# One block of a hybrid encoder on one core: the transfers and gate products of the recurrent branch change engine, and a reciprocal is made in two

## The chip, the core and the metric

The kernel runs on one core of a Trainium2 chip. The time is device microseconds of one launch. A launch computes one layer of a hybrid encoder block for 256 tokens of width 2048, with all weights (some 190 MB in fp32) read once from HBM.

## The reference, cut to what matters

```python
def hybrid_layer(x, mem, ...):
    h = rms_norm(x, norm_g)
    proj = h @ w_in                                  # 256x2048 @ 2048x16512
    (aq, ak, av, az, br, bk, bv, bz, bwd, bad, cq, cz, ga, gb, gc) = split(proj)
    ya = chunked_band_attention(rms_norm(aq), rms_norm(ak), av, a_rel_bias) * silu(az)
    yb = rwkv7_time_mix(br, bk, bv, bwd, bad, ...) * silu(bz)      # 16 heads of 64
    mk, mv = split(rms_norm(mem) @ w_mem_kv)
    yc = memory_cross_attention(rms_norm(cq), rms_norm(mk), mv) * silu(cz)
    merged = sigmoid(ga)*(ya @ w_up_a) + sigmoid(gb)*(yb @ w_up_b) + sigmoid(gc)*(yc @ w_up_c)
    return x + merged @ w_o

def rwkv7_time_mix(...):          # the recurrent branch, per head, over 256 steps
    kk = kk * rsqrt(max(sum(kk*kk), 1e-24))
    # state = state*w_t + (state a_t) b_t + v_t k_t ;  out_t = state r_t
    o = rwkv7_scan(r, decay, k, v, -kk, kk * a)
    o = (o - mean) * rsqrt(var + GN_EPS) * ln_w + ln_b             # per head
    return o + sum(r*k*r_k) * v
```

## The kernel before

**The weight stream.** All weights lie in one HBM array of 186 chunks of 128x2048 fp32 (1 MB). `wload` (L170 to L180) fetches a chunk into a tile `raw` (two buffers) by a DMA that SyncE issues (L175). `wchunk` splits it into two halves and each half into a rounded part and a remainder: ScalarE casts `whi` (L185), VectorE subtracts to get `wlo` (L187); both have four buffers. TensorE then makes twelve matmuls for a half (L204 and L205 with `whi`, L209 with `wlo`; L222, L223 and L225 in the projections that come out transposed). The whole program is 370 such half steps, one after another, and everything else is laid between them.

**The branches as generators.** Attention, cross-attention, transposes and the recurrent branch are Python generators. After each half step `tick()` advances every generator by one yield, so a `yield n` means that the next piece is written n half steps later. The order of the instructions on each engine is then set by a scheduler that sorts all of them; each engine and each engine's DMA queue works its list strictly in that order.

**The recurrent branch** (`rwkv`, L507 to L789) runs for four groups q of four heads. In each:

- L524 to L548: sigmoids of the decay and the learning rate, and ScalarE's square of `kk` into a tile with the tag `tmpA` (one buffer);
- L554 to L559: the norm of `kk`, with a reciprocal over 128x512 on VectorE (L557);
- L577 to L587: the tiles AX, BK and `rk2`;
- L598 to L615: score matmuls, masked into TT;
- L622 and L626: TT goes to an HBM scratch in four DMAs (`scrt`) and comes back as `Tu`, 32x32 triangular systems spread over the partitions;
- L633 to L637: VectorE solves them in 31 steps; L644 and L645 write the result X to HBM twice, L666 to L671 read it back in eight DMAs (D0, D1T and XT, whose tag is `kk`);
- L690 and L699: two small rounds of matmuls; then the state is carried over four chunks c (L712 to L764; L719, L726, L735, L749 are its matmuls, and VectorE copies between them, L721, L729);
- after chunks 1 and 3 the output is normalised per head on GpSimd (L779 to L789). The scale and the shift `lw` come from HBM into a tile of tag `tmpA` (L771) and are read by GpSimd in L785 and L786. L789 adds into `vL`.

All DMAs of this branch but a small weight are issued by SyncE, in one list with the weights. After the branch four products on VectorE (L933 and L934) multiply `vL` by a gate into `zb`, which TensorE transposes (L325).

GpSimd's own DMAs before are the attention bias (L840, 256 rows of 1 KB), the residual input and the output (L954 and L959, 128 rows of 2 KB).

Of the kernel before, what the change touches and what calls it, by code (L numbers as in the profile page):

```python
# [11 lines left out]
ALU = mybir.AluOpType  # L12
# [6 lines left out]
P = 128  # L19
# [74 lines left out]
def _build(ctx, nc, tc, A, out, dbg):  # L94
# [14 lines left out]
    V, SC, G, T = nc.vector, nc.scalar, nc.gpsimd, nc.tensor  # L109
# [8 lines left out]
    def t(pl, shape, tag, dtype=F32, bufs=1):  # L118
        return pl.tile(shape, dtype, name=nm(tag), tag=tag, bufs=bufs)
# [319 lines left out]
    vL = t(vp, [P, 2, 1024], "vL")  # L439
# [36 lines left out]
    rp = pool(rk_st, "rwkv", side="right")  # L476
# [30 lines left out]
    def rwkv(q, w2a2, r_, k_):  # L507
# [44 lines left out]
        rn = t(rp, [P, 2, S], "tmpB")  # L552
# [1 line left out]
        V.tensor_scalar(out=rn2, in0=ssp, scalar1=1e-24, scalar2=None, op0=ALU.max)  # L554
        SC.activation(rn2, rn2, AF.Sqrt)
        yield 2
        V.reciprocal(rn2, rn2)  # L557
        yield 1
        V.tensor_tensor(out=kk, in0=kk, in1=rn, op=ALU.mult)  # L559
        k2 = t(rp, [P, 2, S], "tmpA")  # L560
        for b in range(2):
# [56 lines left out]
        for par in range(2):  # L618
            for b in range(2):
                u0 = (par * 2 + b) * 8  # L620
                r0 = par * 64 + b * 32
                nc.sync.dma_start(scr_t[u0:u0 + 8].rearrange("g s t -> s g t"),  # L622
                                  TT[r0:r0 + 32, :, :, b * 32:b * 32 + 32].rearrange("p b c t -> p (b c) t"))
        yield 1
        Tu = t(rp, [P, 32, 32], "Tu")
        nc.sync.dma_start(Tu.rearrange("p a b -> p (a b)"),  # L626
                          bass.AP(tensor=scr_t.tensor, offset=scr_t.offset, ap=[[1024, 32], [0, 4], [1, 1024]]))
        X = t(rp, [P, 32, 8], "Xu")
        V.tensor_copy(X.rearrange("p a b -> p (a b)"), eye8)
        yield 4  # L630
        tm = t(rp, [P, 192], "tmu")
        for s in range(31):
            n, m = 31 - s, min(s + 1, 8)  # L633
# [7 lines left out]
        V.tensor_copy(Xt, X.rearrange("p a b -> p b a"))  # L641
        scr_x = dr.tile([P, 256], F32, name=nm("scrx"), tag="scrx", bufs=2)
        scr_xt = dr.tile([P, 256], F32, name=nm("scrxt"), tag="scrxt", bufs=2)
        nc.sync.dma_start(scr_x, X.rearrange("p a b -> p (a b)"))  # L644
        nc.sync.dma_start(scr_xt, Xt.rearrange("p a b -> p (a b)"))  # L645

        BKt = t(rp, [P, 2, 3, P], "BKt")
        for b in range(2):
# [2 lines left out]
                T.transpose(bt[:, c, :], BK[:, b, c].rearrange("p a u -> p (a u)"), ident)  # L651
            SC.copy(BKt[:, b], bt)

        yield 1
        XT = t(rp, [P, 8, 64], "kk")
        D0 = t(rp, [P, 8, 32], "D0")
        D1T = t(rp, [P, 8, 32], "D1T")
# [1 line left out]
        for par in range(2):  # L659
            r0 = par * 64  # L660
            ua, ub = par * 16, par * 16 + 8

            def xt_src(u):
                return bass.AP(tensor=scr_xt.tensor, offset=scr_xt.offset + u * 1024, ap=[[32, 32], [1024, 8], [1, 32]])

            nc.sync.dma_start(D0[r0:r0 + 32].rearrange("p g c -> p (g c)"),  # L666
                              bass.AP(tensor=scr_x.tensor, offset=scr_x.offset + ua * 1024,
                                      ap=[[8, 32], [256, 32], [1, 8]]))
            nc.sync.dma_start(D1T[r0:r0 + 32], xt_src(ub))
            nc.sync.dma_start(XT[r0:r0 + 32, :, 0:32], xt_src(ua))  # L670
            nc.sync.dma_start(XT[r0 + 32:r0 + 64, :, 32:64], xt_src(ub))  # L671
        yield 5

        UV = t(rp, [P, 4, 2, 2, 64], "Tu")
        SV = t(rp, [P, 4, 2, 2, 64], "BK")
# [34 lines left out]
        for c in range(4):  # L710
            yield 1
            tt, ro = c // 2, (c % 2) * 64  # L712
            chn = psum([P, 3, 2, 64])
            for b in range(2):
                for par in range(2):
                    rs = slice(par * 64, par * 64 + 64)
                    ot = slice(64 - par * 64, 128 - par * 64)
                    kr = ot if c == 0 else slice(0, P)
                    T.matmul(chn[rs, 0, b, :], AX[kr, b, c, 2 * par, :], SV[kr, c, par, b, :], start=True, stop=True)  # L719
            rhs = t(rp, [P, 2, 64], "rhs")  # L720
            V.tensor_copy(rhs, chn[:, 0])  # L721
            yield 1
            for b in range(2):
                for par in range(2):
                    rs = slice(par * 64, par * 64 + 64)
                    T.matmul(chn[rs, 1, b, :], XT[rs, b * 4 + c, :], rhs[rs, b, :], start=True, stop=True)  # L726
            for par in range(2):
                rs = slice(par * 64, par * 64 + 64)
                V.tensor_copy(UV[rs, c, par], chn[rs, 1])  # L729
            yield 1  # L730
            if c < 3:
                for b in range(2):
                    for par in range(2):
                        rs = slice(par * 64, par * 64 + 64)
                        T.matmul(chn[rs, 2, b, :], BKt[:, b, c, par * 64:par * 64 + 64], UV[:, c, par, b, :],  # L735
                                 start=True, stop=True)
            if c % 2 == 1:
                ob = psum([P, 4, 64])
                for b in range(2):
                    for cc in (c - 1, c):  # L740
                        if cc > 0:
                            oc = slice((cc % 2) * 64, (cc % 2) * 64 + 64)
                            T.matmul(ob[oc, b * 2:b * 2 + 2, :].rearrange("p h i -> p (h i)"), AX[:, b, cc, 1, :],
                                     S0z[cc % 2][:, b].rearrange("p h i -> p (h i)"), start=True, stop=False)
                    for par in range(2):
                        h = b * 2 + par
                        for cc in (c - 1, c):
                            oc = slice((cc % 2) * 64, (cc % 2) * 64 + 64)
                            T.matmul(ob[oc, h, :], RR[:, h, cc, :], UV[:, cc, par, b, :], start=(cc == 0),  # L749
                                     stop=(cc == 0 or par == 1))  # L750
            if c < 3:
                fb = fx[:, :, c].unsqueeze(2).to_broadcast([P, 2, 64])
                t1 = t(rp, [P, 2, 64], "st1")
                if c == 0:
                    V.tensor_copy(t1, chn[:, 2])  # L755
                else:
                    V.tensor_tensor(out=t1, in0=chn[:, 2], in1=S0n, op=ALU.add)
                for par in range(2):
                    rs = slice(par * 64, par * 64 + 64)
                    V.tensor_tensor(out=SV[rs, c + 1, par], in0=t1[rs], in1=fb[rs], op=ALU.mult)  # L760
                    G.tensor_tensor(out=S0z[(c + 1) % 2][rs, :, par], in0=t1[rs], in1=fb[rs], op=ALU.mult)  # L761
                if c < 2:
                    S0n = t(rp, [P, 2, 64], "s0n")
                    G.tensor_tensor(out=S0n, in0=t1, in1=fb, op=ALU.mult)  # L764
            if c % 2 == 1:
                bon = psum([P, 2, P])
                for b in range(2):
                    T.matmul(bon[:, b, :], rk2[:, b, tt * P:tt * P + P], BO, start=True, stop=True)
                lw = t(rp, [P, 2, 256], "tmpA")
                for i in range(2):  # L770
                    nc.sync.dma_start(lw[:, i, :], bass.AP(tensor=A["bc"].tensor, offset=(1 + i) * 1024 + q * 256,  # L771
                                                             ap=[[0, P], [1, 256]]))
                mean = t(sm, [P, 4], "mean", bufs=2)
                V.tensor_reduce(out=mean, in_=ob, axis=AX_X, op=ALU.add)
                V.tensor_scalar(out=mean, in0=mean, scalar1=1.0 / 64, scalar2=None, op0=ALU.mult)
                cen = t(rp, [P, 4, 64], "D0")
                V.tensor_tensor(out=cen, in0=ob, in1=mean.unsqueeze(2).to_broadcast([P, 4, 64]), op=ALU.subtract)
                cq = t(rp, [P, 4, 64], "D1T")
                G.tensor_tensor(out=cq, in0=cen, in1=cen, op=ALU.mult)  # L779
                var = t(sm, [P, 4], "var", bufs=2)  # L780
                V.tensor_reduce(out=var, in_=cq, axis=AX_X, op=ALU.add)
                rsqrt_small(var, var, 4, 1.0 / 64, GN_EPS)
                G.tensor_tensor(out=cen, in0=cen, in1=var.unsqueeze(2).to_broadcast([P, 4, 64]), op=ALU.mult)
                c2 = cen.rearrange("p h i -> p (h i)")
                G.tensor_tensor(out=c2, in0=c2, in1=lw[:, 0, :], op=ALU.mult)  # L785
                G.tensor_tensor(out=c2, in0=c2, in1=lw[:, 1, :], op=ALU.add)  # L786
                bv = t(rp, [P, 256], "M1")
                V.tensor_tensor(out=bv, in0=bon.rearrange("p b s -> p (b s)"), in1=vL[:, tt, tokc], op=ALU.mult)
                G.tensor_tensor(out=vL[:, tt, tokc], in0=c2, in1=bv, op=ALU.add)  # L789
# [140 lines left out]
    finish(rwg)  # L930
    rk_st.close()
    for tt in range(2):
        V.tensor_tensor(out=zb[:, tt, 0:512], in0=vL[:, tt, 0:512], in1=zb0[:, tt, :], op=ALU.mult)  # L933
        V.tensor_tensor(out=zb[:, tt, 512:1024], in0=vL[:, tt, 512:1024], in1=zb[:, tt, 512:1024], op=ALU.mult)  # L934
    dump("y_b", zb)
    g_st = ExitStack()
    gp = pool(g_st, "gb")
# [84 lines left out]
```

## Time and profile before

| | |
|---|---|
| runs of the kernel | 1186.29 us median of 3 (1185.37 to 1188.55) |
| profiled execution | 1184.23 us, span 1182.5 us |
| mean granted TensorE clock | 0.996 of full speed |
| busy: TensorE, VectorE, ScalarE, GpSimd | 1154.7, 778.8, 531.3, 122.5 us |
| moved by DMA | 217.93 MB, 184 GB/s over the span |

The profiled execution lies 1.7 us above its span and 2.1 us under the median of the runs. PE stands for TensorE, DVE for VectorE, ACT for ScalarE, POOL for GpSimd, and SPq for the list of DMAs that SyncE issues. An arrow in a wait reads: who waited, and for what. Small matmuls keep PE counted as busy, so what a stall costs is read from the windows and the waits, not from the share alone.

### The profile page before, as it was taken

To read this page: it belongs to the slowest core of one execution; us is meant where nothing else is said; L and a number is where in the kernel's file an instruction comes from. 1 tells how busy PE (TensorE), PEld (TensorE's weight loads), DVE (VectorE), ACT (ScalarE), POOL (GpSimd) and SP (SyncE) were. 2 spreads that over 40 slices of the span, in tenths; PEclk is the share of its full clock that TensorE was granted. 3 is DMA by queue.
4 is the path that set the end of the run, shared out by engine and by line. 5 is a ranking of instruction groups with operands and counts; after the bars stand their busy time and mean duration, and the time that the engine had idled before them with its cause. 6 is when DMAs were issued, how large, how long until landed. Compare 5 with 4: busy or idle time off the path is not lost.

```text
span 1182.5 us, 15967 instructions
## 1 busy us (share of the span) xinstructions
PE 1154.7 (98%) x6186; PEld 937.2 (79%) x6186; DVE 778.8 (66%) x1320; ACT 531.3 (45%) x655; POOL 122.5 (10%) x170
## 2 busy tenths in 40 slices
PE   7999999999999999999999999998999999999998
PEld 5778888889779777878897778776778777888886
DVE  5584545448969555989675989655789655557543
ACT  6764455445533434344534545532544433444331
POOL 0100000033000022000033100003100004000000
PEclk9999999999999999999999999999999999999999
DMA  8956535465554633564633465544275644544662
GB/s 311 326 214 220 201 122 188 140 211 174 191 199 179 220 117 132 182 240 151 223 126 125 168 217 184 157 148 147 107 245 188 209 156 152 213 178 162 229 218 102
DMA packets 57205, 217.93 MB, mean 184 GB/s; under 512 B 23726, under 2 KB 27566, under 8 KB 33578
## 3 DMA queue, kind: packets, MB, share of 16 engines
q1 hardware_dynamic: 53760, 209.52, 51.2%
q0 software_dynamic: 1440, 4.72, 1.3%
q10 hardware_dynamic: 1930, 2.68, 0.7%
q8 instruction: 48, 0.79, 0.2%
q14 instruction: 27, 0.22, 0.1%
HBM read 212.19 MB, written 3.67 MB: 183 GB/s over the span
## 4 chain that ended last, share of the span: by engine, by line
PE 82%; DVE 5%; DMA 5%; POOL 3%; ACT 2%; issue 2%; SPq 0%; DVEq 0%; POOLq 0%; ACTq 0%
PE pp L204 24%; PE pp L205 23%; PE pp L209 23%; DMA raw<-in_wstream_dram 5%; PE pp L222 2%; PE pp L225 2%; PE pp L223 2%; DVE wlo L187 2%; ACT whi L185 1%; PE ps L325 1%; PE ps L599 1%; PE ps L396 1%; PE ps L420 1%; POOL var L252 1%; DVE tmpB L557 1%
## 5 line engine op out<-in xcount | busy, mean ns | idle before, releaser
L187 DVE TENSOR_TENSOR wlo<-raw,whi 128x1024 fp32r<-128x1024 f32 x370 | 453.0, 1235 | 306.0 <-ACT whi L185 294.7
L185 ACT CAST whi<-raw 128x1024 fp32r<-128x1024 f32 x370 | 383.5, 1049 | 579.5 <-PE pp L205 341.5
L204 PE MATMUL pp<-whi,xh 128*128 128x512 f32 x896 | 363.9, 406 | 0.0
L205 PE MATMUL pp<-whi,xl 128*128 128x512 f32 x896 | 355.8, 397 | 0.0
L209 PE MATMUL pp<-wlo,xh 128*128 128x512 f32 x896 | 246.0, 396 | 4.3 <-DVE wlo L187 4.3
L209 PEld LDWEIGHTS pp<-wlo,xh 128*128 128x128 f32 x896 | 168.5, 188 | 46.4 <-DVE wlo L187 5.6
L204 PEld LDWEIGHTS pp<-whi,xh 128*128 128x128 f32 x896 | 168.7, 188 | 39.8 <-issue 0.7
L205 PEld LDWEIGHTS pp<-whi,xl 128*128 128x128 f32 x896 | 168.9, 188 | 38.2 <-issue 0.5
L204 PE MATMUL pp<-whi,yh 128*128 128x512 f32 x192 | 78.4, 409 | 0.1
L205 PE MATMUL pp<-whi,yl 128*128 128x512 f32 x192 | 76.8, 400 | 0.0
L222 PE MATMUL pp<-xh,whi 128*128 128x256 f32 x272 | 67.3, 286 | 0.0
L223 PE MATMUL pp<-xl,whi 128*128 128x256 f32 x272 | 65.4, 279 | 0.0
L204 PE MATMUL pp<-whi,mh 128*128 128x512 f32 x128 | 52.0, 408 | 8.1 <-ACT mh L275 6.5
L209 PE MATMUL pp<-wlo,yh 128*128 128x512 f32 x192 | 52.6, 395 | 0.0
L222 PEld LDWEIGHTS pp<-xh,whi 128*128 128x128 f32 x272 | 51.0, 188 | 0.6 <-ACT whi L185 0.2
L223 PEld LDWEIGHTS pp<-xl,whi 128*128 128x128 f32 x272 | 51.1, 188 | 0.5 <-issue 0.2
L205 PE MATMUL pp<-whi,ml 128*128 128x512 f32 x128 | 51.2, 401 | 0.0
L205 PE MATMUL pp<-whi,gl 128*128 128x512 f32 x128 | 50.9, 398 | 0.0
L204 PE MATMUL pp<-whi,gh 128*128 128x512 f32 x128 | 50.5, 394 | 0.0
L204 PEld LDWEIGHTS pp<-whi,yh 128*128 128x128 f32 x192 | 36.6, 191 | 9.9 <-ACT whi L185 0.9
L761 POOL TENSOR_TENSOR s0z<-st,fx 64x128 f32<-64x128 f32 x24 | 10.1, 422 | 330.3 <-DVE st L755 292.4
L205 PEld LDWEIGHTS pp<-whi,yl 128*128 128x128 f32 x192 | 36.6, 191 | 8.1
(223 smaller groups left out, 1197.0 us busy)
## 6 DMA issues: line engine op xcount, KB each, us to landing
raw<-in_wstream_dram SPq DMA_DIRECT2D x184, 1024.0 KB, 4.9
xraw<-in_memT_dram SPq DMA_DIRECT2D x8, 256.0 KB, 6.8
tokraw<-in_mem_dram SPq DMA_DIRECT2D x4, 512.0 KB, 6.4
xraw<-in_xT_dram SPq DMA_DIRECT2D x8, 256.0 KB, 7.3
tokraw<-in_x_dram SPq DMA_DIRECT2D x4, 512.0 KB, 6.1
tmpA<-in_bc_dram SPq DMA_DIRECT2D x16, 128.0 KB, 4.4
Tu<-scrt SPq DMA_DIRECT2D x4, 512.0 KB, 5.6
xr<-in_x_dram POOLq DMA_DIRECT2D x8, 256.0 KB, 4.1
```

Source lines behind the costliest of these rows:

```text
L185: SC.copy(hi, sl)
L187: V.tensor_tensor(out=lo, in0=sl, in1=hi.bitcast(F32), op=ALU.subtract)
L204: T.matmul(acc[tt], xh[:, kt + k2, sl], hv[:, k2], start=(kt + k2 == 0), stop=False)
L205: T.matmul(acc[tt], xl[:, kt + k2, sl], hv[:, k2], start=False, stop=False)
L209: T.matmul(acc[tt], xh[:, kt + k2, sl], lv[:, k2], start=False, stop=(last and k2 == 1))
L222: T.matmul(acc, hv[:, k2], xh[:, kt + k2, :], start=(kt + k2 == 0), stop=False)
L223: T.matmul(acc, hv[:, k2], xl[:, kt + k2, :], start=False, stop=False)
L225: T.matmul(acc, lv[:, k2], xh[:, kt + k2, :], start=False, stop=(kt + k2 == 15))
L252: G.tensor_tensor(out=dst, in0=dst, in1=mhalf[:, :n], op=ALU.pow)
L325: T.transpose(bank[:, kk, tt * P:tt * P + P], src[:, tt, (k + kk) * P:(k + kk + 1) * P], ident)
L396: T.matmul(sc[:, tt, :], cqT[:, hh * 2 + k, tt * P:tt * P + P], mkT[:, hd * 2 + k, :], start=(k == 0), stop=(k == 1))
L420: T.matmul(pv[:, tt, :], pT[:, k, tt, :], mv[:, k, hd * 256:(hd + 1) * 256], start=(k == 0), stop=(k == 1))
```

## The change

Four edits. The recurrent branch's transfers of L622, L626, L644, L645 and L666 to L671 are issued by GpSimd. The load of `lw` is made once per group, in place of once for each of chunks 1 and 3; it is issued by ScalarE and written into the program before the state is carried. The four gate products go from VectorE to GpSimd. The reciprocal is made in two pieces of 128x256 with a yield behind each; one yield around the transfer of TT grows from 1 to 2 and one shrinks from 4 to 3, one behind the solve grows from 1 to 2 and the one behind the reads shrinks from 5 to 4.

```diff
-        V.reciprocal(rn2, rn2)
-        yield 1
+        for b in range(2):
+            V.reciprocal(rn[:, b, :], rn[:, b, :])
+            yield 1
...
-                nc.sync.dma_start(scr_t[u0:u0 + 8].rearrange("g s t -> s g t"),
+                nc.gpsimd.dma_start(scr_t[u0:u0 + 8].rearrange("g s t -> s g t"),
...
-        yield 1
+        yield 2
         Tu = t(rp, [P, 32, 32], "Tu")
-        nc.sync.dma_start(Tu.rearrange("p a b -> p (a b)"),
+        nc.gpsimd.dma_start(Tu.rearrange("p a b -> p (a b)"),
...
-        yield 4
+        yield 3
...
-        nc.sync.dma_start(scr_x, X.rearrange("p a b -> p (a b)"))
-        nc.sync.dma_start(scr_xt, Xt.rearrange("p a b -> p (a b)"))
+        nc.gpsimd.dma_start(scr_x, X.rearrange("p a b -> p (a b)"))
+        nc.gpsimd.dma_start(scr_xt, Xt.rearrange("p a b -> p (a b)"))
...
-        yield 1
+        yield 2
         XT = t(rp, [P, 8, 64], "kk")
...
-            nc.sync.dma_start(D0[r0:r0 + 32].rearrange("p g c -> p (g c)"),
+            nc.gpsimd.dma_start(D0[r0:r0 + 32].rearrange("p g c -> p (g c)"),
...
-            nc.sync.dma_start(D1T[r0:r0 + 32], xt_src(ub))
-            nc.sync.dma_start(XT[r0:r0 + 32, :, 0:32], xt_src(ua))
-            nc.sync.dma_start(XT[r0 + 32:r0 + 64, :, 32:64], xt_src(ub))
-        yield 5
+            nc.gpsimd.dma_start(D1T[r0:r0 + 32], xt_src(ub))
+            nc.gpsimd.dma_start(XT[r0:r0 + 32, :, 0:32], xt_src(ua))
+            nc.gpsimd.dma_start(XT[r0 + 32:r0 + 64, :, 32:64], xt_src(ub))
+        yield 4
+        lw = t(rp, [P, 2, 256], "tmpA")
+        for i in range(2):
+            nc.scalar.dma_start(lw[:, i, :], bass.AP(tensor=A["bc"].tensor, offset=(1 + i) * 1024 + q * 256,
+                                                     ap=[[0, P], [1, 256]]))
...
-                lw = t(rp, [P, 2, 256], "tmpA")
-                for i in range(2):
-                    nc.sync.dma_start(lw[:, i, :], bass.AP(tensor=A["bc"].tensor, offset=(1 + i) * 1024 + q * 256,
-                                                             ap=[[0, P], [1, 256]]))
...
-        V.tensor_tensor(out=zb[:, tt, 0:512], in0=vL[:, tt, 0:512], in1=zb0[:, tt, :], op=ALU.mult)
-        V.tensor_tensor(out=zb[:, tt, 512:1024], in0=vL[:, tt, 512:1024], in1=zb[:, tt, 512:1024], op=ALU.mult)
+        G.tensor_tensor(out=zb[:, tt, 0:512], in0=vL[:, tt, 0:512], in1=zb0[:, tt, :], op=ALU.mult)
+        G.tensor_tensor(out=zb[:, tt, 512:1024], in0=vL[:, tt, 512:1024], in1=zb[:, tt, 512:1024], op=ALU.mult)
```

Three places show how the instructions stand. The first is the load of `lw` in the first group. Before, SyncE's list has it twice among the weights; this is the second one, for chunk 3:

```order
L175 DMA raw_3681<-in_wstream_dram 128x2048
L175 DMA raw_3728<-in_wstream_dram 128x2048
L771 DMA tmpA_3766<-in_bc_dram 128x256 x2
L175 DMA raw_3840<-in_wstream_dram 128x2048
L175 DMA raw_3904<-in_wstream_dram 128x2048
```

Now ScalarE's list has it once per group (its line is L676 in the changed program), between two casts of the weights; this is the second group:

```order
L185 CAST whi_4232<-raw_4230 128x1024
L185 CAST whi_4236<-raw_4230 128x1024
L676 DMA tmpA_4800<-in_bc_dram 128x256 x2
L185 CAST whi_4312<-raw_4310 128x1024
L185 CAST whi_4316<-raw_4310 128x1024
```

SyncE's list holds nothing of the branch any more, and the load stands some 50 half steps ahead of its readers.

The second place is ScalarE at the start of the third group (q = 2), where the branch's activations of L524 to L548 and attention's of L285 and L286 stand between the casts. Before:

```order
L524 ACTIVATE sg_5556<-ps_5559,vec_72 128x4x64
L526 ACTIVATE av_5558<-ps_5560,vec_72 128x256
L524 ACTIVATE sg_5556<-ps_5559,vec_72 128x4x64
L526 ACTIVATE av_5558<-ps_5560,vec_72 128x256
L548 ACTIVATE tmpA_5585<-kk_5582 128x512
L185 CAST whi_5651<-raw_5645 128x1024
L537 ACT_TABLE_LOAD
L537 ACTIVATE EP_5575<-cs_5569 128x520
L538 ACTIVATE sg_5576<-cs_5569 128x520
L542 ACTIVATE fx_5579<-fx_5579 128x6
L185 CAST whi_5690<-raw_5688 128x1024
```

Now:

```order
L526 ACTIVATE av_5588<-ps_5590,vec_72 128x256
L548 ACTIVATE tmpA_5615<-kk_5612 128x512
L285 ACTIVATE qn_5631<-pp_5324,rstdx_80 128x512
L537 ACT_TABLE_LOAD
L537 ACTIVATE EP_5605<-cs_5599 128x520
L538 ACTIVATE sg_5606<-cs_5599 128x520
L542 ACTIVATE fx_5609<-fx_5609 128x6
L286 ACTIVATE pp_5324<-pp_5324,rstdx_80 128x512
L285 ACTIVATE qn_5635<-pp_5325,rstdx_80 128x512
L286 ACTIVATE pp_5325<-pp_5325,rstdx_80 128x512
L185 CAST whi_5685<-raw_5679 128x1024
L185 CAST whi_5720<-raw_5718 128x1024
```

One cast that stood behind L548 has moved behind the whole block, and attention's four activations have come in front of it.

The third place is the reciprocal on VectorE in the same group. Before:

```order
L187 TENSOR_TENSOR wlo_5736<-raw_5728,whi_5734 128x1024
L564 SCALAR_TENSOR_TENSOR tmpA_5724<-tmpA_5724,rk_647_3972 128x512
L557 RECIPROCAL tmpB_5669<-tmpB_5669 128x512
L583 TENSOR_TENSOR BK_5752<-tmpA_5724,sg_5576 64x4x64
L559 TENSOR_TENSOR kk_5582<-kk_5582,tmpB_5669 128x512
```

Now (L558 is the reciprocal):

```order
L563 TENSOR_SCALAR tmpA_5783<-av_5588,vec_72 128x256 x2
L565 SCALAR_TENSOR_TENSOR tmpA_5783<-tmpA_5783,rk_646_3970 128x512
L558 RECIPROCAL tmpB_5703<-tmpB_5703 128x256 x2
L187 TENSOR_TENSOR wlo_5764<-raw_5760,whi_5762 128x1024
L187 TENSOR_TENSOR wlo_5768<-raw_5760,whi_5766 128x1024
```

The two pieces stand next to each other, with no `wlo` between them; it is so in all four groups. Two `wlo` have come between the reciprocal and the products that use it.

## Rows read from the trace of the kernel before

**Rows 1.** Page, busy time of each engine: us, share of the span, instructions.
```profile
PE 1154.7 (98%) x6186; PEld 937.2 (79%) x6186; DVE 778.8 (66%) x1320; ACT 531.3 (45%) x655; POOL 122.5 (10%) x170
```

**Rows 2.** Stretches of 30 us: busy time (count) of PE, PEld, DVE, ACT, POOL; granted clock; DMA.
```profile
450.00:480.00 30.00, 27.22 (x204) 23.96 (x203) 18.62 (x35) 13.75 (x19) 6.94 (x11) 0.94 0.39 141
480.00:510.00 30.00, 28.37 (x175) 23.64 (x174) 27.33 (x47) 10.67 (x11) 0.12 (x1) 1.00 0.54 183
...
810.00:840.00 30.00, 26.61 (x141) 19.94 (x140) 12.04 (x23) 13.77 (x19) 6.06 (x10) 0.94 0.31 109
```

**Rows 3.** Waits of PE: us in total, times, longest.
```profile
PE ps L726 <- DVE rhs L721: 7.4, 4, 3.3
...
PE pp L209 <- DVE wlo L187: 5.0, 4, 2.0
...
PE ps L735 <- DVE Tu L729: 1.4, 1, 1.4
```

**Rows 4.** Waits of SyncE's list: us in total, times, longest.
```profile
SPq L771 <- POOL D L786: 43.3, 4, 12.2
```

**Rows 5.** Chain of waits from 440 to 454 us: start, us, what.
```profile
441.21 1.61 POOL D L786
...
442.83 0.33 SPq L771
...
443.74 6.88 DMA raw<-in_wstream_dram
...
452.94 0.29 DVE rhs L721
```

**Rows 6.** One microsecond behind that chain, columns as in Rows 2.
```profile
454.00:455.00 1.00, 1.00 (x3) 0.81 (x4) 0.94 (x4) 0.00 (x0) 0.00 (x0) 0.50 0.00 0
```

**Rows 7.** ACT in order of time, start of the third group: start, us, what, idle before and releaser.
```profile
636.13 1.05 ACT L185 CAST whi<-raw 128x1024 fp32r<-128x1024 f32 x1 [3.12 <-PE pp L205]
...
645.31 0.63 ACT L548 ACTIVATE tmpA<-kk 128x512 f32<-128x512 f32 x1 [3.93 <-POOL D L786]
...
646.90 1.28 ACT L537 ACT_TABLE_LOAD   x1
...
649.36 1.99 ACT L185 CAST whi<-raw 128x1024 fp32r<-128x1024 f32 x2
651.25 0.68 ACT L285 ACTIVATE qn<-pp,rstdx 128x512 f32<-128x512 f32 x1
...
653.54 2.00 ACT L185 CAST whi<-raw 128x1024 fp32r<-128x1024 f32 x2
```

**Rows 8.** Groups by line on POOL: count, busy us, mean ns, idle before.
```profile
L465 POOL TENSOR_TENSOR vL<-vL,vprev 128x512 f32<-128x512 f32 x4 | 7.3, 1832 | 0.0
...
L954 POOL DMA_DIRECT2D xr<-in_x_dram x8 | 4.4, 553 | 8.5 <-issue 4.1 <-DMA out_dram<-xr 4.1 <-POOL vL L789 0.3
...
L840 POOL DMA_DIRECT2D bias<-in_rel_dram x4 | 3.2, 810 | 108.5 <-DVE nmx L858 108.5
```

**Rows 9.** Page, DMA issues: count, KB each, median us to landing.
```profile
Tu<-scrt SPq DMA_DIRECT2D x4, 512.0 KB, 5.6
...
bias<-in_rel_dram POOLq DMA_DIRECT2D x4, 256.0 KB, 3.7
```

**Rows 10.** SyncE's list in order of time, first two groups: start, us from first to last.
```profile
335.03 1.93 SPq L622 DMA_DIRECT2D scrt<-av  x4
...
383.29 0.33 SPq L644 DMA_DIRECT2D scrx<-Xu  x1
...
559.04 0.33 SPq L644 DMA_DIRECT2D scrx<-Xu  x1
```

**Rows 11.** DVE where the first solve starts.
```profile
348.91 0.19 DVE L635 TENSOR_TENSOR tmu<-Tu,Xu 128x31 f32<-128x31 f32 x1 [1.80 <-DMA Tu<-scrt]
```

**Rows 12.** PE, the matmuls that need D0, in the first two groups.
```profile
402.50 0.69 PE L690 MATMUL ps<-D,av 32*32 32x32 f32 x32
...
578.27 0.69 PE L690 MATMUL ps<-D,av 32*32 32x32 f32 x32
```

## The prediction

> **What bounds the kernel now.** The page says it first: TensorE is busy for 1154.7 us of a span of 1182.5, no other engine for more than two thirds [rows 1]. So the time can fall only by what TensorE stands idle, or works at a low clock, about 28 us, much of it at the start and the end, which the change doesn't touch. I read the busy time in stretches of 30 us next. Most stretches in the middle are full; the reader is to see the few that are not. From 450 to 480 us 2.8 us are missing, and from 810 to 840 us 3.4 us, and in both the granted clock is 0.94 in place of 1 [rows 2]. From 480 to 510 us 1.6 us are missing at full clock, with VectorE busy for 27.3 us of the 30 [rows 2].
>
> The waits of TensorE give the holes names. Two kinds are there. Kind A: the small matmuls of the carried state wait for VectorE's copies, L726 for 7.4 us in four waits and L735 for 1.4 us in one, 8.8 us together [rows 3]. Kind B: L209 waits for `wlo`, 5.0 us in four waits [rows 3].
>
> Kind A is not a lack of speed in VectorE. The chain of waits goes back from the copy L721 at 452.94 us to a weight DMA that started at 443.74 and took 6.9 us, from there to the load of `lw` on SyncE's list at 442.83, and from there to GpSimd's L786, which ended at 442.82 [rows 5]. The second `lw` of a group needs the buffer that L786 of the first still reads; while it waits, no weight behind it is asked for. SyncE's list waited there 43.3 us in four waits, one per group [rows 4]. The weights come late, the cast and `wlo` with them, and the copy stands behind `wlo` on VectorE.
>
> Kind A costs more than its idle time. In the microsecond from 454 us the granted clock is 0.50, TensorE's level of 1.2 GHz [rows 6], behind an idle of about 2.8 us. The clock of 0.94 over 30 us is 1.8 us lost, and it is there twice [rows 2]: 3.6 us. Kind B, whose longest wait is 2.0 us [rows 3], shows no such loss from 480 to 510 us [rows 2].
>
> **The change part by part.** Load of `lw`: it is issued once a group, on ScalarE's list, some 50 half steps before it is read, and its buffer's last reader before is VectorE's `rk2`, long done. The wait on SyncE's list is gone and nothing takes its place there. Cost on ScalarE: two issues a group, about 0.3 to 0.5 us each by SyncE's own rows (0.33 us, [rows 5]), beside a ScalarE that is busy for 45% [rows 1]. Saved: all of kind A that rests on late weights, 8.8 + 3.6 = 12.4 us. Part of the L735 wait comes from VectorE's own wait for the last `vL` in the product L934; that product goes to GpSimd, so it is saved as well. From both sides: at least the two deep holes, 2.8 + 3.3 (the longest wait) + 3.6 = 9.7, at most 12.4. I take 12.4.
>
> The four products on GpSimd: a 128x512 product there took 1.83 us [rows 8], so 7.3 us on an engine that is busy for 10% [rows 1]. The first two stand between GpSimd's `Tu` and its write of X, while VectorE solves; the last two follow the last L789, and their reader, the fifth round of transposes, comes several half steps later. I cost them at nothing; if that cover were gone, two of them, 3.7 us, would stand ahead of the transposes.
>
> The reciprocal: both pieces stand next to each other on VectorE in all groups, so its 3.3 us of blockade stays whole. The split itself gives nothing. What it does is to move everything behind it one half step later in each group, and with it the neighbours change. There I expect a loss, in the third group. On ScalarE before, a cast starts at 636.13 us, the square L548 ends at 645.94 behind a wait of 3.93 us for GpSimd, and a cast follows at once [rows 7]. With the new order that cast stands behind the table load and the three activations (646.90 to 649.36 us, 2.46 us) and attention's four activations (651.25 to 653.54, 2.29 us) as well [rows 7]: it starts near 645.9 + 2.5 + 2.3 = 650.7 and ends at 651.7. The cast of 636.13 was released by TensorE's L205, so four halves are in hand then; at the mean of 1182.5 / 370 = 3.2 us a half they last until 636.1 + 12.8 = 648.9. TensorE is late by 2.8 us, and an idle of that length lowered the clock before, 1.8 us more: 4.6 us. Bounds: nothing, if the square comes sooner in the new order, to 2 x 4.6, if the burst on VectorE behind it starves `wlo` too.
>
> The rest of kind B (5.0 us) I halve, to 2.4: in the second group the wait of L548 now stands elsewhere, in the fourth fewer activations share the block, and two `wlo` now come ahead of the products that use the reciprocal. Bounds 0 to 5.0. Kind B after: 4.6 + 2.4 = 7.0, so 2.0 us more than before.
>
> The transfers on GpSimd: per group four of `scrt`, `Tu`, two of X and eight reads, 15 issues. GpSimd issued 128 rows in 553 ns and 256 rows in 810 ns [rows 8], so 2.0 ns a row above some 0.3 us. I estimate from these: a `scrt` transfer has 256 pieces and takes 0.81 us; each D0 has 1024 pieces of 32 B and takes 2.35 us; the other six reads have 256 each. `Tu` first: the first `scrt` goes out at 335.03 us [rows 10]; 4 x 0.81 to issue, 3.7 to land [rows 9], 0.55 to issue `Tu`, 5.6 to land [rows 9] are 13.1 us, and the transfer is written up to one half step (2.8 to 3.2 us) later, so it lands near 351. VectorE began the solve at 348.91, itself after a wait of 1.80 us for it [rows 11]. Some 2 us more of waiting on VectorE; the halves in hand hide that, as they hid the 1.80. Then D0: X goes out at 383.29 us [rows 10] and its matmuls start at 402.50 [rows 12], 19.2 us, and 19.2 in the second group too (559.04 to 578.27). The new order gives one half step more, 22.0. Needed: 1.1 for two issues, 3.7 to land, 2 x 2.35 + 6 x 0.81 = 9.6 for the reads, 3.7 to land: 18.1. Spare are 3.9 us, so nothing on the path. SyncE loses some 70 issues, but it never lacked time for them: no gain there beyond kind A.
>
> Sum: 1184.2 - 12.4 + 2.0 = 1173.8 us for an execution like the profiled one. That one was 2.1 us under the median of the runs, so 1176 for a median.
>
> **A rule of the skill.** The Trainium skill, page "SBUF — State Buffer", in its box on the trap "DVE blocks DMA", says that a DMA issued by GpSimd has its descriptors written by GpSimd's cores, which can't write while VectorE holds the shared port in its fast mode, and gives 620 ns for a transfer alone against 3100 beside such work. It speaks against this change. The rows of GpSimd's own transfers [rows 8] stand at 553 and 810 ns, close to the figure for a transfer alone, with VectorE working beside them; but there were 12 such loads, none within a solve. By the trace the sum stays; by the rule it is the last rival below.
>
> **The rivals.**
> First: nothing is given back. The square comes early enough, the block of the third group costs no more than before, and kind B falls to 2.4: 1184.2 - 12.4 - 2.6 = 1169.2, for the median 1171. For it: the weights run ahead where SyncE no longer stops. Against it: only two `raw` buffers, so the lead is soon that of before.
>
> Second: the denser blocks take all of it. If in each of the last three groups a cast is late as reckoned for the third, 3 x 4.6 = 13.8 stand in place of 5.0: 1184.2 - 12.4 + 8.8 = 1180.6, for the median 1183. For it: kind B exists in the trace and is at its worst where VectorE is nearly full [rows 2]. Against it: the order has the long block in the third group alone.
>
> Third, slower: GpSimd is too slow with small pieces. The spare 3.9 us over 3584 pieces (2 x 1024 + 6 x 256) are used up at 2.0 + 1.1 = 3.1 ns a piece; each nanosecond beyond that holds TensorE at L690 for 3.6 us a group. At 6 ns it is 10.4 us in each of the first two groups, 20.8, and with a clock loss of 1.8 each 24.4: 1173.8 + 24.4 = 1198, for the median 1200. The gain is lost from 4.5 ns on. Five times the price, as the box would have it, 10 ns, is 24.7 us in each of the two: 1227 or more. For it: no transfer with pieces under 1 KB was issued by GpSimd in this trace, and the solve is a train of short work on VectorE. Against it: the only two measured prices lie 2 ns a row apart, and even a third more would leave TensorE untouched.
>
> **How the numbers follow.** The forecast has 0.60, the first rival 0.20, the second 0.10, the third 0.10. What can be told from no change is 0.3%, 3.6 us: 1182.7 to 1189.9. Faster are the forecast and the first rival, 0.80. The second ends at the border and stands for the same, 0.09, the remaining 0.01 being its worse half with the third: slower 0.11. The range reaches below to the first rival with both of its ends (kind A 12.4, kind B gone: 1168.9 for the median, so 1168) and above to the second with 2 x 4.6 in the third group: 1173.8 + 9.2 = 1183.0, for the median 1185, so 1186. Only the third rival and the tails lie outside. The forecast's own range is 1172 to 1181: 2.7 above for the lower bound of kind A and 2.4 for kind B unhalved; 4.6 below for a third group without loss.
>
> **What would show it.** Right: SyncE's list waits for `wlo` alone; the stretches at the end of each group are full and the clock stays at 1; L726 and L735 no longer wait for copies; the new loss is a wait of about 3 us near the start of the third group, behind ScalarE's block, with the clock at 0.5 behind it; the reciprocals follow each other without a gap. The price on GpSimd: D0's issue near 2.35 us and a `scrt` near 0.8. Wrong: TensorE waiting at L690 or VectorE for long at the first product of a solve (GpSimd's transfers); L726 still waiting (then it was not `lw`); no wait in the third group (the first rival).

## The result and the profile after

The changed kernel takes 1178.0 us (median of 4 runs, 1176.42 to 1179.34) against 1185.85 us (4 runs). The ratio is 0.994, 95% interval 0.9921 to 0.9959: faster by 0.4 to 0.8%. 1176 was forecast. The profiled execution took 1177.95 us with a span of 1175.9 us, 6.6 us under the span before; the forecast for such an execution was 1173.8.

The same stretches of 30 us as in [rows 2], and one more (columns as there):

```profile
450.00:480.00 30.00, 30.00 (x241) 26.68 (x239) 24.08 (x42) 15.79 (x20) 7.40 (x13) 1.00 0.48 162
480.00:510.00 30.00, 30.00 (x170) 24.72 (x169) 24.01 (x42) 11.97 (x14) 0.12 (x1) 1.00 0.54 184
660.00:690.00 30.00, 26.52 (x117) 20.60 (x117) 25.51 (x35) 10.40 (x13) 2.22 (x3) 0.94 0.56 186
750.00:780.00 30.00, 27.76 (x157) 22.64 (x157) 16.51 (x22) 16.03 (x25) 0.00 (x0) 0.94 0.48 164
810.00:840.00 30.00, 30.00 (x182) 22.75 (x181) 16.25 (x33) 12.15 (x18) 13.32 (x19) 1.00 0.39 137
```

The holes of before are full. Two new ones stand where the third group starts (660 to 690 us) and where it meets attention (750 to 780 us), each with a granted clock of 0.94. TensorE's waits answer to [rows 3]:

```profile
PE pp L209 <- DVE wlo L187: 4.3, 4, 2.5
PE ps L876 <- ACT apT L872: 2.2, 1, 2.2
...
PE ps L870 <- ACT apr L863: 0.5, 1, 0.5
```

No copy of the carried state is waited for any more, and nothing on SyncE's list waits for GpSimd: [rows 4] has no counterpart. In the third group the longest wait is this one, in order of time on TensorE, with the microsecond behind it:

```profile
664.33 1.20 PE L209 MATMUL pp<-wlo,xh 128*128 128x512 f32 x4 [1.03 <-DVE wlo L187]
678.68 2.08 PE L209 MATMUL pp<-wlo,xh 128*128 128x512 f32 x4 [2.45 <-DVE wlo L187]
```

```profile
679.00:680.00 1.00, 1.00 (x3) 0.81 (x3) 0.97 (x2) 0.00 (x0) 0.00 (x0) 0.50 0.00 0
```

The wait that was told right behind ScalarE's block is not there. The cast behind the block starts where it was told to, at 650.66 us, but TensorE has work until 656.7 us and then waits for 0.3 us only. The two waits shown above come much later. The first stands behind the reciprocal on VectorE, the second behind a cast that waited for its weights; VectorE had freed their buffer only at 671.2 us.

```profile
650.66 2.95 ACT L185 CAST whi<-raw 128x1024 fp32r<-128x1024 f32 x3
...
676.18 1.99 ACT L185 CAST whi<-raw 128x1024 fp32r<-128x1024 f32 x2 [3.53 <-DMA raw<-in_wstream_dram]
```

```profile
659.84 3.36 DVE L558 RECIPROCAL tmpB<-tmpB 128x256 f32<-128x256 f32 x2
663.11 2.29 DVE L187 TENSOR_TENSOR wlo<-raw,whi 128x1024 fp32r<-128x1024 f32 x2
```

GpSimd's transfers, by line (count, busy us, mean ns, idle before), answer to [rows 8]:

```profile
L623 POOL DMA_DIRECT2D scrt<-av x16 | 9.8, 616 | 100.1 <-DVE av L608 100.1
...
L667 POOL DMA_DIRECT2D D<-scrx x8 | 6.4, 806 | 6.9 <-DMA scrx<-Xu 6.9
...
L670 POOL DMA_DIRECT2D D1T<-scrxt x8 | 4.7, 593 | 0.0
```

A read of 1024 pieces takes 806 ns and one of 256 takes 593: 0.28 ns a piece, not 2.0. And the first product of the solve, which answers to [rows 11], stands here in the first and the third group:

```profile
350.69 0.19 DVE L636 TENSOR_TENSOR tmu<-Tu,Xu 128x31 f32<-128x31 f32 x1 [2.28 <-DMA Tu<-scrt]
...
708.22 0.19 DVE L636 TENSOR_TENSOR tmu<-Tu,Xu 128x31 f32<-128x31 f32 x1 [2.64 <-DMA Tu<-scrt]
```

### The profile page after: what moved, and what is told of

Same layout as the page of the kernel before. It is cut to its first block, busy times and chain, and to the rows that moved or that the text cites. A ratio compares the mean times of both kernels' runs of the same rounds, so it can differ in the third digit from the quotient of the medians.

```text
span 1175.9 us, 15987 instructions
## 1 busy us (share of the span) xinstructions
PE 1155.9 (98%) x6186; PEld 938.6 (80%) x6186; DVE 784.1 (67%) x1320; ACT 528.3 (45%) x654; POOL 164.2 (14%) x234
## 4 chain that ended last, share of the span: by engine, by line
PE 85%; DVE 5%; DMA 5%; ACT 2%; issue 2%; POOL 1%; SPq 0%; DVEq 0%; ACTq 0%; POOLq 0%
PE pp L204 23%; PE pp L209 23%; PE pp L205 23%; DMA raw<-in_wstream_dram 4%; PE pp L222 3%; PE pp L225 3%; PE pp L223 3%; DVE wlo L187 2%; ACT whi L185 1%; PE ps L325 1%; PE ps L600 1%; PE ps L420 1%; PE ps L396 1%; PE ps L724 1%; PE ps L731 1%
## 5 line engine op out<-in xcount | busy, mean ns | idle before, releaser
L209 PE MATMUL pp<-wlo,xh 128*128 128x512 f32 x896 | 246.5, 397 | 3.8 <-DVE wlo L187 3.8
L209 PEld LDWEIGHTS pp<-wlo,xh 128*128 128x128 f32 x896 | 168.5, 188 | 45.7 <-DVE wlo L187 5.1
L209 PE MATMUL pp<-wlo,yh 128*128 128x512 f32 x192 | 52.6, 395 | 0.0
L209 PEld LDWEIGHTS pp<-wlo,yh 128*128 128x128 f32 x192 | 36.1, 188 | 8.7
```

The lines of the kernel that those rows point to most:

```text
L209: T.matmul(acc[tt], xh[:, kt + k2, sl], lv[:, k2], start=False, stop=(last and k2 == 1))
```

## The experiments

Each ratio is that of a kernel to the kernel before, timed beside it on the same chip (its median lay between 1184.1 and 1185.5 us there). Lines in the expectations are those of the kernel that is spoken of.

**The parts, one by one.** (The products on GpSimd were not run alone.) First `lw` alone:

```diff
-                lw = t(rp, [P, 2, 256], "tmpA")      # after chunks 1 and 3
-                    nc.sync.dma_start(lw[:, i, :], ...)
...
         yield 5
+        lw = t(rp, [P, 2, 256], "tmpA")              # once, ahead of the state
+            nc.scalar.dma_start(lw[:, i, :], ...)
```

> The kernel before with one edit: lw is loaded once a group, by ScalarE, ahead of the state. Theory (the wait for lw on SyncE's list is the whole gain, the rest of the change gives nothing or costs): SyncE's list waits for weights' buffers alone, L726 and L735 no longer wait for copies, the clock no longer falls near 455 and 819 us, time 1186 - 12 = 1174 us (1172 to 1176), below the changed kernel's 1178. Rival (the transfers on GpSimd carry part of the gain): about half, 1179 to 1182.

1174.3 us, ratio 0.9925 (0.9895 to 0.9954), span 1170.8. TensorE no longer waits at L726, and the two stretches with a clock of 0.94 are at 1.00. The wait of 1.4 us at L735 stays (it is L739 here). The span fell by 11.7 us, where 12.4 were reckoned with that wait and 11.0 without it. This one edit does all that the whole change does, or more.

Then GpSimd's transfers alone (`nc.gpsimd` for `nc.sync` in L622 to L671, all yields as before):

> The kernel before with one edit: the branch's transfers of L622 to L671 are issued by GpSimd, lw stays on SyncE's list. Theory: within 2 us of the kernel before, 1184 to 1188 us, with SyncE's list still waiting some 43 us for L786 and L726 waiting for its copies. Rival (SyncE's list free of 60 issues lets the weights run earlier): 4 us or more faster, 1182 or less.

1188.8 us, ratio 1.0044 (1.0029 to 1.006): slower, which neither side had. SyncE's list waits for L786 as before:

```profile
SPq L771 <- POOL D L786: 43.3, 4, 12.2
```

Set half step against half step (by the starts of TensorE's L209 and L225), the two executions stay within 1 us of each other until 728 us; between there and 772 us the new one loses 4.4 us. That is where the third group meets attention.

The changed kernel with the reciprocal in one piece and its one yield:

> The changed kernel with the reciprocal in one piece and one yield, as before. Theory (the extra half step packs ScalarE's activations and VectorE's burst in the third group, and delays attention near 750 us): the waits near 664 and 679 us shrink to less than 1 us together and the clock stays up there, 1178 - 5 = 1173 us (1171 to 1175). Rival (those waits come from the weights' new rhythm, not from the split): 1177 to 1179.

1180.7 us, ratio 0.9968 (0.9953 to 0.9983). The wait near 679 went, and 0.6 us is left near 663, as the theory said, but the time did not fall: it is rather higher than the changed kernel's 0.994, though the two intervals touch. The holes of kind B are all back (1.6 us near 486, 2.0 near 845), and between 724 and 766 us 6.1 us are lost against the kernel with `lw` alone. Neither way told that.

The reciprocal in two, alone:

```diff
-        V.reciprocal(rn2, rn2)
-        yield 1
+        for b in range(2):
+            V.reciprocal(rn[:, b, :], rn[:, b, :])
+            yield 1
```

> The kernel before with one edit: the reciprocal in two pieces with a yield behind each. Theory: the waits for lw stay and the third group's block is added: 1186 + 4 = 1190 us (1188 to 1193). Rival (the split is neutral by itself): 1185 to 1187. A third way, that the pieces let a wlo in between them: the wait of L209 near 491 us goes, 1183 to 1185.

1174.8 us, ratio 0.9918 (0.9895 to 0.9941). All three ways missed it: this gains as much as `lw` alone. Yet SyncE's list still waits for GpSimd:

```profile
SPq L772 <- POOL D L787: 38.1, 4, 11.3
```

The reason stands beside the wait. A chunk can be asked for when the last `wlo` of an older chunk has freed its buffer; in the median over all chunks the list asks 0.03 us after that `wlo`. Before, that `wlo` started at 437.25 us and the list went on to the next weights at 443.74, 5.3 us after the buffer was free:

```profile
437.25 1.22 DVE L187 TENSOR_TENSOR wlo<-raw,whi 128x1024 fp32r<-128x1024 f32 x1
```

With the split, that `wlo` starts at 444.61, and the list goes on at 447.78, 1.5 us after its end:

```profile
444.61 1.63 DVE L187 TENSOR_TENSOR wlo<-raw,whi 128x1024 fp32r<-128x1024 f32 x1 [1.91 <-ACT whi L185]
```

```profile
446.86 0.80 SPq L772 DMA_DIRECT2D tmpA<-in_bc_dram  x2
447.78 0.36 SPq L175 DMA_DIRECT2D raw<-in_wstream_dram  x1
```

Most of a wait for `lw` is time in which the list would have waited for a buffer anyway. Only what lies behind the buffer's freeing makes weights late: 5.3, 4.1, 5.4 and 4.4 us in the four groups before, 1.5, 3.0, 1.5 and 4.4 with the split. A chunk is two half steps, and the split moves the groups by 1, 2, 3 and 4 of them; an odd count moves the wait from one half of a chunk to the other. In the fourth group, moved by four, the holes of before are still there (1.4 and 0.6 us). Lateness is not yet loss: in this kernel the list is also 5.2 us late at 935 us, behind the reads, and TensorE waits for nothing there.

**Is it the half step?** Two kernels leave the reciprocal whole:

```diff
         V.reciprocal(rn2, rn2)
-        yield 1
+        yield 2        # in the second kernel: yield 3
```

> The kernel before with yield 2 in place of yield 1 behind the reciprocal, which stays in one piece. Theory (the split works through its extra half step alone: it moves the wait for lw by a half step in each group, and so to another place within a weight chunk of two halves): as the split alone, 1173 to 1177 us, weights asked for 1 to 3 us after their buffer is free in the first three groups. Rival (the two pieces help): 1184 to 1187.

> The kernel before with yield 3 there, two extra half steps a group. Theory (each group is moved by an even count of halves, so the wait for lw falls at the same place in a chunk as before): SyncE's list asks for the next chunk 4 to 5 us after its buffer is free in all four groups and L726 waits again: 1181 to 1187 us. Rival (any later start helps): 1172 to 1177.

One more half step: 1175.2 us, ratio 0.9915 (0.9892 to 0.9938), as the split. Its weights are asked for 1.5, 5.0, 1.5 and 4.4 us late: the first and the third group as told, not the second, where L726 waits 1.2 us. Two more: 1179.9 us, ratio 0.9952 (0.9933 to 0.9971), under the range that was told, but with the delays back at 5.3, 3.0, 5.3 and 4.4 us (the second group lower than was told) and the wait of before with them:

```profile
PE ps L726 <- DVE rhs L721: 7.7, 4, 3.7
```

```profile
450.00:480.00 30.00, 26.30 (x205) 23.20 (x199) 16.75 (x33) 10.63 (x15) 8.05 (x13) 0.94 0.41 129
660.00:690.00 30.00, 29.07 (x128) 22.86 (x128) 25.62 (x37) 16.12 (x20) 2.88 (x3) 1.00 0.40 146
810.00:840.00 30.00, 27.00 (x186) 20.26 (x185) 17.27 (x33) 8.63 (x10) 9.12 (x14) 0.94 0.43 135
```

What it gains is elsewhere: kind B is down from 5.0 to 1.6 us, and a wait of 1.4 us for attention's L871 is gone. So the two pieces do nothing, and the extra half step does all. That it works by where the wait falls within a chunk fits three groups of four. In the second the lateness was 4.1 us before, 3.0 and 5.0 us with the group moved by two half steps and 3.0 with four, and what sets it there was not found.

**Do `lw` and the split add?**

> The kernel with lw alone moved, and the reciprocal in two with its yields. Theory (split and lw fill the same holes near 453, 633 and 817 us, and the split brings the waits of the third group): the gains of 9 and 9 don't add, 1173 to 1177 us. Rival (the split has a gain of its own): 1165 to 1168.

1173.8 us, ratio 0.9905 (0.9885 to 0.9925): they don't. Both fill the same holes.

**Which transfer costs?** `lw` alone moved, with one kind of transfer on GpSimd or the other:

> The kernel with lw alone moved (1174.3 us), and besides the transfers of TT and Tu (L622, L626) issued by GpSimd. The scheduler then sets the solve one wlo earlier in VectorE's list in the first, third and fourth group. Theory (that place is the cost of the GpSimd transfers: VectorE waits for Tu with a wlo queued behind it, and attention's work near 720 to 760 us comes late): 1178 to 1181 us, VectorE's waits for Tu 8 us in place of 3.7, TensorE waiting at L869 and L875. Rival (the cost lies in the reads behind the solve): 1173 to 1176.

> The kernel with lw alone moved (1174.3 us), and besides the writes of X and the eight reads (L644 to L671) issued by GpSimd; the solve stands in VectorE's list where it stood. Theory: no difference, 1173 to 1176 us, no wait at L690. Rival (the reads land later from GpSimd's list and hold the branch up): 1178 to 1181.

1175.9 us (0.9917, 0.9897 to 0.9937) and 1175.4 us (0.9916, 0.9896 to 0.9937): by itself neither costs anything that can be told. The theory on the solve's place failed as it stood, though VectorE did wait 8.3 us for Tu. That wait isn't GpSimd's alone: with Tu back on SyncE, in the kernel that follows, it is 7.2 us. Then the changed kernel itself, with only TT and Tu back on SyncE:

```diff
-                nc.gpsimd.dma_start(scr_t[u0:u0 + 8].rearrange("g s t -> s g t"),
+                nc.sync.dma_start(scr_t[u0:u0 + 8].rearrange("g s t -> s g t"),
-        nc.gpsimd.dma_start(Tu.rearrange("p a b -> p (a b)"),
+        nc.sync.dma_start(Tu.rearrange("p a b -> p (a b)"),
```

> The changed kernel with the transfers of TT and Tu (L623, L627) back on SyncE, the writes of X and the reads still on GpSimd. Theory (the GpSimd transfers cost only where both kinds are there, since together they delay VectorE's list and a weight chunk in the third group): the waits near 749 and 755 us and the low clock behind them go, 1173 to 1175 us against 1178. Rival (the loss there comes from the reads alone, or from the split): 1177 to 1179.

1172.3 us, ratio 0.9892 (0.9869 to 0.9914), against 0.994 (0.9921 to 0.9959) for the changed kernel. The two executions are 1.6 us apart at 728 us, most of it from the start and the clock near 680, and lose 4.0 us more against each other by 774. VectorE shows why. In the changed kernel all copies that follow the solve stand ahead of a `wlo` and of attention's L854:

```profile
744.12 1.77 DVE L688 COPY Tu<-vL 64x128 f32<-64x128 f32 x8
745.93 1.23 DVE L187 TENSOR_TENSOR wlo<-raw,whi 128x1024 fp32r<-128x1024 f32 x1
747.07 0.28 DVE L854 SCALAR_TENSOR_TENSOR apr<-ps,bias 128x128 f32<-128x128 f32 x1
```

With Tu on SyncE's list, the `wlo` and attention come after the first of these copies:

```profile
741.68 0.22 DVE L688 COPY Tu<-vL 64x128 f32<-64x128 f32 x1
741.94 1.23 DVE L187 TENSOR_TENSOR wlo<-raw,whi 128x1024 fp32r<-128x1024 f32 x1
743.08 0.28 DVE L854 SCALAR_TENSOR_TENSOR apr<-ps,bias 128x128 f32<-128x128 f32 x1
...
745.96 1.24 DVE L688 COPY Tu<-vL 64x128 f32<-64x128 f32 x6
```

ScalarE's exponential waits 6.5 us in the one and 4.9 in the other, and TensorE's wait at L876 is 2.2 us in the one and 0.8 in the other. In the kernel without the split VectorE's order is another, and there the chain that led to the wait began with a weight chunk that took 7.7 us from issue to landing, beside GpSimd's reads:

```profile
732.58 7.71 DMA raw<-in_wstream_dram
740.39 1.06 ACT whi L185
```

But the reads of GpSimd are not needed for such a chunk. In the kernel before, with all of the branch on SyncE, a chunk at that place took 7.9 us (from 734.2 us), and in the last kernel of this part, with all of it on SyncE as well, the chain that leads to the same wait begins with one of 7.3 us (from 729.3 us). So the order is shown for the changed kernel; by what way both kinds of transfer cost 4 to 6 us where the split is not made stays open.

The change's other yields (2, 3, 2 and 4 around the transfers) were not tried by themselves. The kernel with TT and Tu back on SyncE has them all, and at 0.9892 it is not slower than `lw` and the split without them (0.9905).

**A better version.** `lw` moved, and kept in two tiles that lie idle until the next solve (its two readers changed to match); the products on GpSimd; nothing else:

```diff
+        lw = [t(rp, [P, 32, 8], "Xu"), t(rp, [P, 8, 32], "tmx")]
+        for i in range(2):
+            nc.scalar.dma_start(lw[i].rearrange("p a b -> p (a b)"), ...)
...
```

> The kernel with lw alone moved, lw now in the buffers of X and its transpose, which nothing needs until the next solve, so that L548 needn't wait for GpSimd's L786; and the four gate products on GpSimd. Theory (the holes at the start of a group, near 487 and 839 us, come from ScalarE's wait at L548): these shrink by half or more, and L735's wait of 1.4 us goes: 1169 to 1171 us. Rival (they come from VectorE's burst around the reciprocal): the 1.4 us alone, 1172 to 1174.

1168.1 us, ratio 0.9853 (0.983 to 0.9875), better than both kernels and a little better than expected. L548 waits for GpSimd no longer, and kind B is gone:

```profile
PE pp L209 <- DVE wlo L187: 0.3, 1, 0.3
```

```profile
480.00:510.00 30.00, 30.00 (x165) 24.52 (x164) 26.07 (x49) 11.72 (x13) 0.12 (x1) 1.00 0.62 215
```

VectorE is busy for 26.1 us of these 30, nearly as before (27.3), with its reciprocal whole: its burst alone was not the cause; with ScalarE's wait gone, the hole is gone. With the split added:

> The kernel with lw moved into the buffers of X and the products on GpSimd (1168.1 us), and besides the reciprocal in two with its yields. Theory (the split's only effect that is left is the packed block on ScalarE in the third group): slower than without it, 1170 to 1173 us, with a wait near 660 to 680. Rival (with L548's wait gone the block starts early enough): 1167 to 1169.

1174.5 us, ratio 0.9908 (0.9887 to 0.9929): the extra half step costs 6 us here, where no wait for `lw` is left for it to move. As told it waits near 663 and 679 us (0.6 and 1.0). More lies between 750 and 780: 1.8 us of clock and a wait of 2.2 at attention's L877, where the kernel without the split waits 1.9 us at full clock; and a wait of 1.2 us at L741 near 601 us is new. The hole at L877 is that of the changed kernel (2.2 us at L876 and the same clock), with no transfer of the branch on GpSimd.

## Why the prediction came out as it did

- *Kind A, 12.4 us saved.* Right in cause and size: with `lw` alone the waits at L726 and both low clocks, 11.0 of the 12.4 us, are gone, and the span fell by 11.7. By the runs the saving is 0.75% (0.46 to 1.05), 5 to 12 us. But the wait of 43.3 us on SyncE's list was read as if it all counted. Of it some 19 us (5.3 + 4.1 + 5.4 + 4.4) lay behind a free buffer; so a shift by a half step could cure three of the holes as well, which the prediction did not see. (The load ran some 40 half steps ahead of its first reader, not 50; and the wait of 2.0 us in kind B stands near 850 us, not in the stretch from 480 us, with the clock at 1.00 there too.)
- *The split gives nothing itself and packs the third group, 4.6 us.* The pieces did nothing, and the cast behind the block was late as reckoned (650.66 us for 650.7). But TensorE did not run out of halves at 648.9 us: the branch's small matmuls, 2.8 us from 636.9 us on, lay between them, and they lasted until 651.0. The loss came 14 and 28 us after that cast, as waits near 664 and 679 us, 3.5 us and some 1.8 of clock, with `wlo` held up on VectorE and the weights behind it. The prediction had that only as its upper bound ("if the burst on VectorE behind it starves `wlo` too"), so that 5.3 us came where 4.6 were reckoned is in part luck. The rest of kind B shrank further than the 2.4 reckoned, to 0.8 of the 4.3 us of waits at L209 that are left. Kind B after came to 6.1 us where 7.0 were forecast. What was missed is the other side: alone, the half step is worth as much as `lw`.
- *GpSimd's transfers at nothing.* This step failed, and it is why the gain is not larger. The price of an issue was put too high (2.35 us for a D0 where 0.81 came), Tu was told to land near 351 us and the solve began at 350.7, and L690 never waited. The third rival is refuted. The loss came from what the prediction named and waved off, "the halves in hand hide that": in three groups they did. In the third, attention's work stands behind the solve on VectorE, and 4 to 6 us went there, clock included, in all three kernels with both kinds of transfer on GpSimd and in none of the three with one kind. The hole is not theirs alone: in the last kernel the extra half step brings it, without them. What costs is how the work around that place falls, and these transfers are one of the things that shift it.
- *The products on GpSimd at nothing.* A small gain, which the prediction had booked under kind A: the wait of 1.4 us at L735 near the end of the fourth group is in each of the nine kernels with the products on VectorE and in none of the five with them on GpSimd (1294 and 1374 ns each there).
- *Sum.* 10.4 us forecast for a profiled execution, 6.3 measured: kind A as told, kind B 1 us better than told, and some 4 us lost where the third group meets attention, of which nothing was told. Some 1.3 us more stand between the two executions after their first 100 us, ahead of the branch's transfers.
- *The rule of the skill.* The Trainium skill, "SBUF — State Buffer", box "DVE blocks DMA", with the figures in the section behind it, would have a transfer from GpSimd take five times as long beside VectorE. It says so of a VectorE op in a two-port mode, as a copy of fp32 from SBUF to SBUF is. The trace puts that to the test in part only. The 16 `scrt` issues lasted 584 to 832 ns, but no copy ran beside them. Reads and writes of X that ran beside copies of `vL` (0.22 us each) were stretched little: 862 ns at most for a D0, where 784 is the least. No long copy ran beside an issue here.

## What to carry to other kernels

A wait on a queue costs only what lies behind the moment at which the queue could have gone on; look for that moment (here the freeing of a buffer) before the whole wait is booked. Where work is laid between the steps of a stream, one step more or less can undo or bring a stall by its phase alone, so test an edit without the yield that comes with it. And moving a transfer to another engine can move the order of everything else: here that cost more than any issue did.

## What the runs showed of the hardware

The clock did not answer to a stall's length alone. The idle of 2.45 us near 678 us stands in the changed kernel and in the one with Tu on SyncE; in the first the granted clock fell to 0.50 behind it, in the second, shown here, it stayed at 1.00:

```profile
678.00:679.00 1.00, 0.55 (x2) 0.49 (x3) 1.00 (x2) 0.00 (x0) 0.00 (x0) 1.00 0.00 0
679.00:680.00 1.00, 1.00 (x6) 0.80 (x5) 0.97 (x3) 0.00 (x0) 0.00 (x0) 1.00 0.00 0
```

A wait of 2.05 us did likewise: behind the one near 850 us in the kernel before the clock stayed at 1.00, behind the one near 845 us in the changed kernel without the split it was 0.94 over 840 to 870 us. What parts them was not found. Small pieces were cheap for GpSimd to issue: 0.21 us for 768 more of them, at the same 32 KB.
